# Sums on every partition by one product with ones, and a power of all elements on POOL, in two norms of a hybrid layer

## The chip, the cores and the metric

The kernel runs on one core of a Trainium2 chip. A time is the device time of one execution in microseconds (us); the number quoted for a kernel is the median of its runs. One further execution of the kernel was recorded by the hardware profiler, and every row below is from that one. The engines go by the names of the profile: PE is the matrix engine (PEld its weight load), DVE the vector engine, ACT the scalar engine, POOL the GpSimd engine, SP the engine that issues the weight DMAs.

## The reference, cut to what matters

One step of a layer with two mixers and an MLP, on 16 meta, 256 prompt and 64 sample tokens, D_MODEL = 2048. Two norms are touched by the change:

```python
def _rmsnorm(x, w):
    xf = x.astype(jnp.float32)
    xf = xf * lax.rsqrt(jnp.mean(xf * xf, axis=-1, keepdims=True) + EPS)
    return (xf * w.astype(jnp.float32)).astype(x.dtype)

# in _layer: the gated norm of the SSD mixer, one mean for each token and each of 4 groups of 512
ya = ya.reshape(b, l, SSD_D_INNER) * jax.nn.silu(z_a.astype(f32))
ya = _rmsnorm(ya.reshape(b, l, SSD_GROUPS, -1), ssd_norm_w.reshape(SSD_GROUPS, -1)).reshape(b, l, SSD_D_INNER)
...
# the norm ahead of the MLP, one mean for each token over 2048
hid = jnp.square(jax.nn.relu(_rmsnorm(h, norm_mlp_w) @ w_up))
h = h + hid @ w_down
```

## The kernel before, in words

Activations lie with channels on the 128 partitions and tokens along the free dimension. The weights, most of the 340.57 MB that the kernel reads, stream through once, in chunks of 512 rows by 256 columns. For each chunk `wsplit` (L201) makes two rounded halves: ACT copies the chunk to `hi`, DVE subtracts to get `lo`. `block` (L213) then runs 24 products on PE for the chunk (8 tiles, three products each: hi by x-high, hi by x-low, lo by x-high). `raw`, `hi` and `lo` have three buffers each, so the halves of a chunk can be made once the chunk three places earlier is used up, and two chunks lie ready ahead of PE at the most. Results go to `pbig`, a PSUM pool of four banks; a block fills two of them.

PE's order is written out by hand (L73). `run` (L240) interleaves a main generator (projections: the weight stream) with a side generator (scans and norms): what the side yields is the stretch of main work, in us, that PE does before it goes on with the side. The other engines' order is fixed when the kernel is built: a list planner takes, of the instructions that are ready by its own prices, the one that is earliest in the program. On the chip each engine runs its queue strictly in that order.

**The group norm.** `scan_ssd` (L608) runs for four groups, each beside the projections of the next. It goes through three chunks of tokens (64, 128 and 128 output tokens, c = 0, 1, 2). For a chunk it makes decay factors `em` (DVE, ACT, then POOL multiplies by `cb`), the state update (`xw` and `xwr` on DVE, `ph` on PE) and the output `yz` (`pyd` on PE). Then come squares (`sq`), which POOL adds up to one [128, tokens] tile, a yield, and `rstd_bcast` (L594). There PE sums over the partitions with a product by one column of ones, so that the tokens come to lie on the partitions and the sum is one column; DVE scales it; POOL raises this one column to -0.5 (L600); DVE multiplies the identity by it (L602, `dg`). A second yield follows, and PE spreads the diagonal over all partitions by a product with ones (`prb`). DVE then scales the four tiles of `yz` from PSUM (L67), ACT and DVE write `yh` and `yl`, the operands of the output projection. The yields place the next chunk's products (`pcb`, `pxt`, `ph`, `pyd`) at fixed distances behind.

**The MLP norm.** `mlp_rstd` (L1094) runs beside `mlp_first`, the first two blocks of the up projection, which fill all four `pbig` banks. It sums squares in `h2`, and does the same as above for three sets of 128 tokens: six PE passes, a power of a [128, 4] tile, three diagonals, six PE passes, and an ACT copy to `rbc` [128, 320]. `hidden` (L1132) then reads `pbig` and `rbc` on DVE (`hf`), and this is what frees a bank for the third block.

`conv` (L397), which runs for the projections of x, B, C, q, k and v, has short copies on POOL, products on DVE and copies on ACT.

Of the kernel before, what the change touches and what calls it, by code (L numbers as in the profile page):

```python
# [8 lines left out]
F32 = mybir.dt.float32  # L9
F32R = mybir.dt.float32r  # L10
AF = mybir.ActivationFunctionType
ALU = mybir.AluOpType
AX = mybir.AxisListType

P = 128
D = 2048
# [6 lines left out]
NO = NPR + NSA  # L23
DFF = 4 * D
EPS = 1e-6
# [17 lines left out]
def tile_hybrid_step(ctx: ExitStack, tc: tile.TileContext, i: dict, o: dict):  # L43
# [10 lines left out]
    def scr(name):  # L54
        return pss.tile([P, 512], F32, tag="sc", name=name)

    def mm(out, lhsT, rhs, start=True, stop=True, **kw):
        nc.tensor.matmul(out, lhsT=lhsT, rhs=rhs, start=start, stop=stop, **kw)  # L58

    def act(out, in_, func=AF.Copy, **kw):  # L60
        nc.scalar.activation(out=out, in_=in_, func=func, **kw)  # L61

    def tt(eng, out, a, b, op):
        eng.tensor_tensor(out=out, in0=a, in1=b, op=op)  # L64
# [4 lines left out]
    V, G = nc.vector, nc.gpsimd  # L69
    MUL, ADD, SUB = ALU.mult, ALU.add, ALU.subtract  # L70
# [5 lines left out]
    ident = const.tile([P, P], F32, name="ident")  # L76
    make_identity(nc, ident)
    ones = const.tile([P, P], F32, name="ones")
# [3 lines left out]
    nhalf_pow = const.tile([P, 4], F32, name="nhalf_pow")  # L82
    G.memset(nhalf_pow, -0.5)

    def transp(out, in_):
        n = in_.shape[0]
        nc.tensor.transpose(out, in_, ident[:n, :n])
# [418 lines left out]
    for n in range(2):  # L506
        w, wr = wt[:, n * 8:(n + 1) * 8, :], wpool.tile([P, 8, P], F32R, tag="hi", name="wtr", bufs=3)
# [83 lines left out]
    def new_y():  # L591
        return (cpool.tile([P, 4, NO], F32R, tag="yh", name="yh"), cpool.tile([P, 4, NO], F32R, tag="yl", name="yl"))

    def rstd_bcast(pool, ssum, n, width, wait):  # L594

        pc = scr("prs")
        mm(pc[:n, 256:257], ssum[:, :n], ones[:, 0:1])
        r = pool.tile([P, 1], F32, tag="r1", name="r1", bufs=2)
        V.tensor_scalar(out=r[:n], in0=pc[:n, 256:257], scalar1=1.0 / width, scalar2=EPS, op0=MUL, op1=ADD)
        tt(G, r[:n], r[:n], nhalf_pow[:n, 0:1], ALU.pow)  # L600
        dg = pool.tile([P, P], F32, tag="dg", name="dg", bufs=2)
        V.tensor_scalar(out=dg[:n, :n], in0=ident[:n, :n], scalar1=r[:n, 0:1], scalar2=None, op0=MUL)  # L602
        yield wait
        pr = scr("prb")
        mm(pr[:, :n], ones[:n, :], dg[:n, :n])
        return pr[:, :n]

    def scan_ssd(g, sg, x4, bc, z4):  # L608
        gh = slice(g * 8, (g + 1) * 8)
# [15 lines left out]
        ps = scr("psi")  # L625
# [8 lines left out]
        for c in range(3):  # L634
            lo, n, l0, nl, o0 = CH_LO[c], CH_N[c], L_LO[c], L_N[c], O_LO[c]
# [3 lines left out]
            ps = scr("pcb")  # L639
# [6 lines left out]
            pcb, ps = ps, scr("pxt")  # L646
# [39 lines left out]
            if c:  # L686
                po = scr("pyo")
                pov = po.rearrange("p (t l) -> p t l", l=nl)
                for t in range(4):
                    w = slice(t * P, (t + 1) * P)  # L690
# [17 lines left out]
                tt(V, yz[:, :, :nl], yz[:, :, :nl], pd, ADD)  # L708

            tt(G, yz[:, :, :nl], yz[:, :, :nl], z4[:, :, o0:o0 + nl], MUL)  # L710
            nx = max(nl, 96)
            sq = sg.tile([P, 4, P], F32, tag="sq", name="sq", bufs=1)
            if nl < nx:
                G.memset(sq[:, 0, nl:nx], 0.0)
            act(sq[:, :, :nl], yz[:, :, :nl], AF.Square)
            tt(G, sq[:, 0:2, :nl], sq[:, 0:2, :nl], sq[:, 2:4, :nl], ADD)
            tt(G, sq[:, 0, :nl], sq[:, 0, :nl], sq[:, 1, :nl], ADD)
            yield (5.4, 7.6, 7.0)[c]
            rb = yield from rstd_bcast(sg, sq[:, 0, :], nx, 512, (3.2, 5.2, 3.6)[c])
            rb = rb[:, :nl]  # L720
            yh, yl = ys[g] = ys.get(g) or new_y()
            for t in range(4):
                stt(yz[:, t, :nl], yz[:, t, :nl], par[:, SN + g * 4 + t:SN + g * 4 + t + 1], rb, MUL, MUL)
            act(yh[:, :, o0:o0 + nl], yz[:, :, :nl])
            tt(V, yl[:, :, o0:o0 + nl], yz[:, :, :nl], yh[:, :, o0:o0 + nl].bitcast(F32), SUB)
            if c == 2:
                for h, dst in zip(new, (o["ssd_p"], o["ssd_s"])):
                    ps = scr("pso")
                    for t in range(4):
                        transp(ps[:, t * P:(t + 1) * P], h[:, t * P:(t + 1) * P])  # L730
                    st = sg.tile([P, 4, P], F32, tag="sio", name="sio", bufs=2)
                    act(st, ps)
                    nc.sync.dma_start(dst[0, 0, gh].rearrange("(t h) p n -> (h p) t n", h=2), st)
                    yield 1.0
# [322 lines left out]
    with ExitStack() as sctx:  # L1057
        sg = sctx.enter_context(tc.tile_pool(name="sg", bufs=1))
        run(kept(proj_ssd(1), tiles), scan_ssd(0, sg, *tiles[0]))
        run(chain(out_a(0), kept(proj_ssd(2), tiles)), scan_ssd(1, sg, *tiles[1]))  # L1060
        run(chain(out_a(1), kept(proj_ssd(3), tiles)), scan_ssd(2, sg, *tiles[2]))
        run(chain(out_a(2), kept(proj_gdn(0), tiles)), scan_ssd(3, sg, *tiles[3]))
    with ExitStack() as sctx:
        sg = sctx.enter_context(tc.tile_pool(name="sgg", bufs=1))
# [6 lines left out]
        h2 = const.tile([P, NO], F32, name="h2")  # L1071
# [19 lines left out]
    mp = ctx.enter_context(tc.tile_pool(name="mp", bufs=1))  # L1091
    rbc = mp.tile([P, NO], F32, name="rbc")

    def mlp_rstd():  # L1094

        toks = ((0, 0), (128, 0), (192, 64))
        yield 5.0
        for k in range(KD):
            q = h2 if k == 0 else mp.tile([P, NO], F32, tag="hf", name="q", bufs=3)
            act(q, acc[:, k, :], AF.Square)  # L1100
            if k:
                tt(V, h2, h2, q, ADD)
            yield 0.9
        pc = scr("prs")
        r = mp.tile([P, 4], F32, name="rm")
        G.memset(r, 1.0)
        for n, (t0, _) in enumerate(toks):
            mm(pc[:, n:n + 1], h2[:, t0:t0 + P], ones[:, 0:1])
        V.tensor_scalar(out=r[:, 0:3], in0=pc[:, 0:3], scalar1=1.0 / D, scalar2=EPS, op0=MUL, op1=ADD)
        tt(G, r, r, nhalf_pow, ALU.pow)  # L1110
        pr = scr("prb")
        yield 3.5
        for n, (t0, d) in enumerate(toks):
            dg = mp.tile([P, P], F32, tag="dg", name="dg", bufs=3)
            V.tensor_scalar(out=dg, in0=ident, scalar1=r[:, n:n + 1], scalar2=None, op0=MUL)
            mm(pr[:, t0 + d:t0 + P], ones, dg[:, d:])
        act(rbc, pr[:, :NO])

    def conv_states():
        for r in range(6):  # L1120
# [35 lines left out]
    toks = ((0, slice(0, P), 0), (P, slice(0, P), P), (192, slice(64, P), 256))  # L1156
# [32 lines left out]
    for q in range(NQ):  # L1189
        hid[q] = (mp.tile([P, 16, NO], F32R, tag="hh", name="hh"), mp.tile([P, 16, NO], F32R, tag="hl", name="hl"))  # L1190
        pts = []
        if q == 0:
            run(kept(mlp_first(), pts), mlp_rstd())
            pts = pts[0]
        for b in range(8):
            if b >= len(pts):
                run(kept(mlp_up(), pts), conv_states() if q == 0 and b == 4 else None)
            hidden(q, b, pts[b])
        if q == NQ - 1:
            final_tiles()  # L1200
        for b in range(8):
            last = q == NQ - 1 and b
            run(mlp_down(q, b), chain(final_cols(b - 1), *([final_sum()] if b == 7 else [])) if last else None)
    H = D // 2
    with tc.manual_schedule():
        for t in range(3):
            final_part(7, t)
            r, n = frs[:, t:t + 1], toks[t][1]
            stt(r[n], fss[n, t, 7:8], 1.0 / D, fsum[n, t:t + 1], MUL, ADD)
            tt(G, r[n], r[n], nhalf_pow[n, 0:1], ALU.pow)  # L1210
        for m in range(2):
            for t, (_, n, t0) in enumerate(toks):
                dst = o["y_prompt"][0, t0:t0 + P, :] if t < 2 else o["y_sample"][0]
                w, r = slice(m * H, (m + 1) * H), frs[n, t:t + 1]
# [36 lines left out]
```

## Time and profile before

| | |
|---|---|
| median of 3 runs | 2333.14 us (2331.46 to 2334.69) |
| the profiled execution | 2331.78 us |
| its span, from the first to the last instruction | 2330.1 us |
| PE busy | 2300.5 us (99%), granted clock 0.994 of full speed |
| DVE busy | 1360.9 us (58%) |
| ACT busy | 1064.6 us (46%) |
| POOL busy | 333.0 us (14%) |
| HBM read | 340.57 MB, 155 GB/s with the writes over the span |

How to read it: matmuls overlap in their pipeline, so a busy PE says that it was not waiting, not that it could not be faster. Busy shares are means over stages: in the SSD stage (120 to 525 us) DVE and POOL have far more to do than in the MLP (1410 us to the end). Idle time of an engine costs nothing unless PE waits for it. "[2.3 <-DVE c]" behind a row is the idle time ahead of it and what ended it.

### The profile page before, as it was taken

Reading aid. Unit: us, or ns where it says so; the run is one execution under the profiler, and the core shown is the slowest. Engines: PE = TensorE matmul, PEld = TensorE weight load, DVE = VectorE, ACT = ScalarE, POOL = GpSimd, SP = SyncE. Lnnn points to the kernel's source line nnn. Section 1 sums busy time; section 2 is a strip of 40 time slices with the busy share of each in tenths; the row PEclk is TensorE's granted clock in tenths of the full one; section 3 lists DMA queues with packets and bytes.
Section 4 is the critical chain, followed back from the end, with each engine's and each line's share of the span. In section 5 each row is a group of like instructions: output and inputs, shape, how many; then the busy total and the mean of one; then the engine's idle time right before and its main releaser. Section 6 shows DMA issues by size and latency. Waiting matters only on the chain.

```text
span 2330.1 us, 40632 instructions
## 1 busy us (share of the span) xinstructions
PE 2300.5 (99%) x16393; PEld 2278.1 (98%) x16393; DVE 1360.9 (58%) x2147; ACT 1064.6 (46%) x1830; POOL 333.0 (14%) x488
## 2 busy tenths in 40 slices
PE   7999999999999999999999999999999999999997
PEld 7999999999999999999999999999999999999997
DVE  6674858585865547658668467444444444444444
ACT  5655546455445545554554445433343244324433
POOL 3151505041211102212212110000000000000000
PEclk8999999999999999999999999999999999999999
DMA  7846555545575555555546644544554444445543
GB/s 194 225 121 188 143 159 150 159 135 173 156 200 170 148 164 139 154 150 144 156 148 165 170 142 145 154 149 151 148 154 149 150 148 151 154 146 153 168 141 117
DMA packets 411046, 362.87 MB, mean 156 GB/s; under 512 B 48329, under 2 KB 407834, under 8 KB 410394
## 3 DMA queue, kind: packets, MB, share of 16 engines
q1 hardware_dynamic: 410746, 360.15, 53.1%
q8 instruction: 128, 2.10, 0.4%
q14 instruction: 60, 0.49, 0.1%
q10 hardware_dynamic: 112, 0.13, 0.0%
HBM read 340.57 MB, written 19.66 MB: 155 GB/s over the span
## 4 chain that ended last, share of the span: by engine, by line
PE 91%; DVE 5%; DMA 2%; issue 1%; SPq 1%; ACT 0%; ACTq 0%; POOL 0%; DVEq 0%
PE pbig L58 84%; DVE lo L64 1%; PE po L58 1%; DMA em<-rowd 1%; DVE pr L64 1%; DVE ubt L858 1%; PE pS L58 0%; PE pw L58 0%; PE pyd L58 0%; DVE c L67 0%; PE pkk L58 0%; PE pqk L58 0%; PE ph L58 0%; DMA x<-in_x_sample_dram 0%; PE pyo L58 0%
## 5 line engine op out<-in xcount | busy, mean ns | idle before, releaser
L64 DVE TENSOR_TENSOR lo<-raw,hi 128x1024 fp32r<-128x1024 f32 x591 | 739.1, 1251 | 697.3 <-ACT hi L61 688.0
L61 ACT ACTIVATE hi<-raw 128x1024 fp32r<-128x1024 f32 x592 | 626.3, 1058 | 892.1 <-PE pbig L58 834.6
L58 PE MATMUL pbig<-uh,hi 128*128 128x320 f32 (+2 forms) x2176 | 688.9, 317 | 3.1 <-ACT uh L61 3.1
L58 PE MATMUL pbig<-ul,hi 128*128 128x320 f32 (+2 forms) x2176 | 681.9, 313 | 2.9 <-DVE ul L67 2.7
L58 PE MATMUL pbig<-uh,lo 128*128 128x320 f32 (+2 forms) x2176 | 680.8, 313 | 1.6 <-DVE lo L64 1.6
L58 PEld LDWEIGHTS pbig<-uh,hi 128*128 128x128 f32 x2176 | 410.9, 189 | 9.1 <-ACT uh L61 3.8
L58 PEld LDWEIGHTS pbig<-ul,hi 128*128 128x128 f32 x2176 | 410.8, 189 | 4.7 <-DVE ul L67 4.3
L58 PEld LDWEIGHTS pbig<-uh,lo 128*128 128x128 f32 x2176 | 411.0, 189 | 2.4 <-DVE lo L64 2.4
L58 PE MATMUL pbig<-hh,hi 128*128 128x320 f32 x1024 | 318.0, 311 | 0.0
L58 PE MATMUL pbig<-hnl,hi 128*128 128x320 f32 x1024 | 317.1, 310 | 0.0
L58 PE MATMUL pbig<-hl,hi 128*128 128x320 f32 x1024 | 316.3, 309 | 0.0
L58 PE MATMUL pbig<-hh,lo 128*128 128x320 f32 x1024 | 316.2, 309 | 0.0
L58 PE MATMUL pbig<-hnh,lo 128*128 128x320 f32 x1024 | 315.8, 308 | 0.0
L58 PE MATMUL pbig<-hnh,hi 128*128 128x320 f32 x1024 | 315.1, 308 | 0.0
L58 PEld LDWEIGHTS pbig<-hnh,lo 128*128 128x128 f32 x1024 | 192.9, 188 | 0.0
L58 PEld LDWEIGHTS pbig<-hl,hi 128*128 128x128 f32 x1024 | 192.6, 188 | 0.0
L58 PEld LDWEIGHTS pbig<-hh,hi 128*128 128x128 f32 x1024 | 192.6, 188 | 0.0
L58 PEld LDWEIGHTS pbig<-hnh,hi 128*128 128x128 f32 x1024 | 192.4, 188 | 0.2
L58 PEld LDWEIGHTS pbig<-hh,lo 128*128 128x128 f32 x1024 | 192.5, 188 | 0.0
L58 PEld LDWEIGHTS pbig<-hnl,hi 128*128 128x128 f32 x1024 | 192.2, 188 | 0.0
L58 PE MATMUL pbig<-yh,hi 128*128 128x320 f32 x512 | 161.1, 315 | 0.0
L58 PE MATMUL pbig<-yh,lo 128*128 128x320 f32 x512 | 157.5, 308 | 0.0
(303 smaller groups left out, 2425.8 us busy)
## 6 DMA issues: line engine op xcount, KB each, us to landing
raw<-in_w_in_dram SPq DMA_DIRECT2D x256, 512.0 KB, 3.8
raw<-in_w_up_dram SPq DMA_DIRECT2D x128, 512.0 KB, 3.8
raw<-in_w_down_dram SPq DMA_DIRECT2D x128, 512.0 KB, 3.4
raw<-in_w_out_dram SPq DMA_DIRECT2D x64, 512.0 KB, 3.4
raw<-in_w_in_dram SPq DMA_DIRECT2D x32, 256.0 KB, 3.1
em<-rowd SPq DMA_DIRECT2D x8, 512.0 KB
u<-uD SPq DMA_DIRECT2D x4, 768.0 KB, 7.1
eab<-rowd SPq DMA_DIRECT2D x8, 336.0 KB, 6.9
```

The lines of the kernel that those rows point to most:

```text
L58: nc.tensor.matmul(out, lhsT=lhsT, rhs=rhs, start=start, stop=stop, **kw)
L61: nc.scalar.activation(out=out, in_=in_, func=func, **kw)
L64: eng.tensor_tensor(out=out, in0=a, in1=b, op=op)
L858: V.tensor_reduce(out=ubt[:NE, j0:, s], in_=v, axis=AX.X, op=ADD)
```

## The change

`rstd_bcast` becomes `rstd`. One product with the full 128 x 128 matrix of ones leaves the sum of each token on every partition at once, as a [128, tokens] tile in PSUM. DVE scales it and adds EPS into SBUF, and POOL raises all its elements to -0.5. The diagonal, the second product, the yield between them and the memset that padded 64 tokens to 96 are gone; DVE reads the factor from SBUF and not from PSUM. The second yield is kept, behind the writes of `yh` and `yl`. The MLP norm calls the same function for 320 tokens; its three sums, three diagonals, the yield of 3.5 and the ACT copy are gone.

```diff
-    def rstd_bcast(pool, ssum, n, width, wait):
-
-        pc = scr("prs")
-        mm(pc[:n, 256:257], ssum[:, :n], ones[:, 0:1])
-        r = pool.tile([P, 1], F32, tag="r1", name="r1", bufs=2)
-        V.tensor_scalar(out=r[:n], in0=pc[:n, 256:257], scalar1=1.0 / width, scalar2=EPS, op0=MUL, op1=ADD)
-        tt(G, r[:n], r[:n], nhalf_pow[:n, 0:1], ALU.pow)
-        dg = pool.tile([P, P], F32, tag="dg", name="dg", bufs=2)
-        V.tensor_scalar(out=dg[:n, :n], in0=ident[:n, :n], scalar1=r[:n, 0:1], scalar2=None, op0=MUL)
-        yield wait
-        pr = scr("prb")
-        mm(pr[:, :n], ones[:n, :], dg[:n, :n])
-        return pr[:, :n]
+    def rstd(out, sums, width):
+
+        w = sums.shape[1]
+        ps = scr("prb")
+        mm(ps[:, :w], ones, sums)
+        V.tensor_scalar(out=out, in0=ps[:, :w], scalar1=1.0 / width, scalar2=EPS, op0=MUL, op1=ADD)
+        tt(G, out, out, nhalf_pow[:, 0:1].to_broadcast([P, w]), ALU.pow)
...
             yield (5.4, 7.6, 7.0)[c]
-            rb = yield from rstd_bcast(sg, sq[:, 0, :], nx, 512, (3.2, 5.2, 3.6)[c])
-            rb = rb[:, :nl]
+            rb = sg.tile([P, P], F32, tag="dg", name="rb", bufs=2)[:, :nl]
+            rstd(rb, sq[:, 0, :nl], 512)
             yh, yl = ys[g] = ys.get(g) or new_y()
             for t in range(4):
                 stt(yz[:, t, :nl], yz[:, t, :nl], par[:, SN + g * 4 + t:SN + g * 4 + t + 1], rb, MUL, MUL)
             act(yh[:, :, o0:o0 + nl], yz[:, :, :nl])
             tt(V, yl[:, :, o0:o0 + nl], yz[:, :, :nl], yh[:, :, o0:o0 + nl].bitcast(F32), SUB)
+            yield (3.2, 5.2, 3.6)[c]
...
-        pc = scr("prs")
-        r = mp.tile([P, 4], F32, name="rm")
-        G.memset(r, 1.0)
-        for n, (t0, _) in enumerate(toks):
-            mm(pc[:, n:n + 1], h2[:, t0:t0 + P], ones[:, 0:1])
-        V.tensor_scalar(out=r[:, 0:3], in0=pc[:, 0:3], scalar1=1.0 / D, scalar2=EPS, op0=MUL, op1=ADD)
-        tt(G, r, r, nhalf_pow, ALU.pow)
-        pr = scr("prb")
-        yield 3.5
-        for n, (t0, d) in enumerate(toks):
-            dg = mp.tile([P, P], F32, tag="dg", name="dg", bufs=3)
-            V.tensor_scalar(out=dg, in0=ident, scalar1=r[:, n:n + 1], scalar2=None, op0=MUL)
-            mm(pr[:, t0 + d:t0 + P], ones, dg[:, d:])
-        act(rbc, pr[:, :NO])
+        rstd(rbc, h2, D)
```

## Rows read from the trace of the kernel before

**Rows 1.** The page: busy share of PE, and the chain by engine.
```profile
PE 2300.5 (99%) x16393; PEld 2278.1 (98%) x16393; DVE 1360.9 (58%) x2147; ACT 1064.6 (46%) x1830; POOL 333.0 (14%) x488
...
PE 91%; DVE 5%; DMA 2%; issue 1%; SPq 1%; ACT 0%; ACTq 0%; POOL 0%; DVEq 0%
```

**Rows 2.** POOL's groups by form: count | busy us, mean ns | idle before, releaser.
```profile
L64 POOL TENSOR_TENSOR sq<-sq 128x128 f32<-128x128 f32 x12 | 6.0, 499 | 2.4 <-ACT sq L61 2.1
...
L64 POOL TENSOR_TENSOR r<-r,nhalf_pow 128x1 f32<-128x1 f32 x8 | 4.4, 551 | 10.6 <-DVE r L599 10.4
...
L64 POOL TENSOR_TENSOR rm<-rm,nhalf_pow 128x4 f32<-128x4 f32 x1 | 1.0, 1014 | 20.4 <-DVE rm L1109 20.4
```

**Rows 3.** DVE's waits: waiter, releaser, us in total, times, longest.
```profile
DVE lo L64 <- ACT hi L61: 688.0, 424, 8.1
...
DVE on L64 <- POOL so L64: 10.2, 9, 1.2
...
DVE dg L602 <- POOL r L64: 5.6, 9, 0.7
```

**Rows 4.** Timeline of POOL, groups 0 and 1: start, us, instruction.
```profile
190.20 0.56 POOL L64 TENSOR_TENSOR r<-r,nhalf_pow 128x1 f32<-128x1 f32 x1 [0.38 <-DVE r L599]
...
235.53 0.55 POOL L64 TENSOR_TENSOR r<-r,nhalf_pow 96x1 f32<-96x1 f32 x1 [4.65 <-DVE r L599]
...
259.44 0.55 POOL L64 TENSOR_TENSOR r<-r,nhalf_pow 128x1 f32<-128x1 f32 x1 [2.53 <-DVE r L599]
...
271.85 3.53 POOL L64 TENSOR_TENSOR em<-em,cb 128x512 f32<-128x512 f32 x2
...
290.17 0.55 POOL L64 TENSOR_TENSOR r<-r,nhalf_pow 128x1 f32<-128x1 f32 x1
```

**Rows 5.** Timeline of DVE, group 1, around the three norms.
```profile
237.47 1.23 DVE L64 TENSOR_TENSOR lo<-raw,hi 128x1024 fp32r<-128x1024 f32 x1 [1.09 <-ACT hi L61]
...
260.94 2.36 DVE L64 TENSOR_TENSOR lo<-raw,hi 128x1024 fp32r<-128x1024 f32 x2 [0.63 <-ACT hi L61]
...
266.88 1.11 DVE L67 SCALAR_TENSOR_TENSOR yz<-yz,par,prb 128x128 f32<-128x128 f32 x4
...
292.13 1.22 DVE L64 TENSOR_TENSOR lo<-raw,hi 128x1024 fp32r<-128x1024 f32 x1
```

**Rows 6.** Timeline of ACT, group 1: splits that begin where PE ends a chunk.
```profile
243.67 1.06 ACT L61 ACTIVATE hi<-raw 128x1024 fp32r<-128x1024 f32 x1 [2.74 <-PE pbig L58]
...
264.49 1.06 ACT L61 ACTIVATE hi<-raw 128x1024 fp32r<-128x1024 f32 x1 [0.48 <-PE pbig L58]
...
298.59 1.06 ACT L61 ACTIVATE hi<-raw 128x1024 fp32r<-128x1024 f32 x1 [0.37 <-ACT z L61]
```

**Rows 7.** Timeline of DVE at the MLP norm.
```profile
1431.84 0.16 DVE L1109 TENSOR_SCALAR rm<-prs 128x3 f32<-128x3 f32 x1 [2.42 <-PE prs L58]
...
1437.04 1.28 DVE L67 SCALAR_TENSOR_TENSOR hf<-pbig,rbc 128x320 f32<-128x320 f32 x3
```

**Rows 8.** Timeline of PE at the MLP norm: the sums.
```profile
1431.00 0.72 PE L58 MATMUL prs<-ones,h 128*128 128x1 f32 x6
```

**Rows 9.** Timeline of ACT in the MLP: the split at a chunk's end.
```profile
1442.49 1.06 ACT L61 ACTIVATE hi<-raw 128x1024 fp32r<-128x1024 f32 x1 [0.81 <-PE pbig L58]
```

**Rows 10.** The chain in order of time: its longest piece in the MLP.
```profile
1474.39 740.14 PE pbig L58 x5055
```

**Rows 11.** Windows at the start: PE, PEld, DVE, ACT, POOL busy, PEclk, DMA, GB/s.
```profile
40.00:44.00 4.00, 3.25 (x11) 2.71 (x11) 2.11 (x5) 2.11 (x5) 0.00 (x0) 0.50 1.13 214
44.00:48.00 4.00, 3.09 (x18) 2.91 (x17) 1.35 (x3) 1.55 (x4) 0.52 (x2) 0.84 1.09 274
```

**Rows 12.** Timeline of PE: a stall ahead of these windows, and two products of groups 0, 1.
```profile
37.10 0.42 PE L58 MATMUL pbig<-ul,hi 128*128 128x336 f32 x1 [2.07 <-DVE ul L67]
...
199.47 0.30 PE L58 MATMUL pbig<-yh,hi 128*128 128x320 f32 x1
...
278.90 1.04 PE L58 MATMUL pyd<-em,xt 128*64 128x128 f32 x16
```

More of the change, by code (lines that the diff above doesn't have):

```diff
@@ L710, in scan_ssd @@
             tt(G, yz[:, :, :nl], yz[:, :, :nl], z4[:, :, o0:o0 + nl], MUL)
-            nx = max(nl, 96)
             sq = sg.tile([P, 4, P], F32, tag="sq", name="sq", bufs=1)
-            if nl < nx:
-                G.memset(sq[:, 0, nl:nx], 0.0)
             act(sq[:, :, :nl], yz[:, :, :nl], AF.Square)
@@ L1094, in mlp_rstd @@
     def mlp_rstd():
-        toks = ((0, 0), (128, 0), (192, 64))
         yield 5.0
```

## The prediction

> **What bounds the kernel now.** I read the page's busy shares and chain first. PE is busy for 99% of the span and is 91% of the chain that ended last [rows 1]: the kernel runs as fast as PE gets its operands, and whatever makes PE wait is paid in full. PE is fed by DVE and ACT, which split each weight chunk shortly before it is used. In the table of waits, DVE sits idle for 688 us ahead of `lo`, and all of that ends with ACT's `hi` [rows 3], which itself starts when PE frees a buffer. So the splitters are ahead, but only by the two chunks that three buffers allow. That is the cover that any new wait on DVE has, and the reader is to keep it in mind: a few us, not tens.
>
> **POOL's power, the new cost.** Next I read POOL's groups by form. The power of one column takes 551 ns, that of four columns 1014 ns, both on 128 partitions [rows 2]. The difference is 463 ns for three columns: 154 ns a column, and 397 ns that don't depend on the width. The add of 128 columns on the same engine takes 499 ns, at most 3.9 ns a column, so it is the power itself that is slow. The change raises 64, 128, 128 columns in each of four groups, and 320 once. No row shows a power wider than 4 columns, so both ends are kept: along the line of the two rows 64 columns take 10.3 us, 128 take 20.1 us and 320 take 49.8 us; at the price of the add they take 0.5 us or less, and 1.25 us for 320. I take the line, since its rows are of this very operation, and since work that has to be repeated for each column is what a steady 154 ns looks like.
>
> The Trainium skill speaks against this: GPSIMD Engine Reference, section "Elementwise — side-by-side cycle accounting", puts a two-input elementwise operation at about 2.6 cycles an element at 1.2 GHz, whatever it computes. By that, as an estimate, the powers would take about 0.3 us for 128 columns and 0.7 us for 320, and the sum would end as in the last rival below. The trace agrees for the add (499 ns) and not for the power (551 to 1014 ns for three columns more); the measurement decides.
>
> **Who waits for it.** The four scalings of `yz` on DVE read the result. What stands between them and the scaling of the sums in DVE's queue is set by the planner's price for a power. The waits show that this price is low: of the results that DVE waits for from POOL, the powers are the ones. `on` waits 10.2 us in 9 of 12 cases, 1.1 us each, and `dg` 5.6 us in 9 of 12 [rows 3], each about the whole of the power ahead of it; the planner put nothing between. So I expect the scalings right behind, and DVE standing still for nearly all of the power. Behind them in DVE's queue are the next `lo` (PE waits for it), the products of `conv`, and the next chunk's `xw` and `xwr` (PE's `ph`). Behind the power on POOL are the next chunk's `em` by `cb` (PE's `pyd`) and the short copies of `conv`. ACT's `yh` waits too, with `hi` behind it.
>
> **The group norm, priced in group 1.** A chunk is due at PE when PE ends the one before it, and that instant is seen where ACT begins a later `hi`.
> - 64 columns: the power starts at 235.5 [rows 4] and ends at 245.8. With about 0.9 us for four scalings and 1.2 us for the next `lo`, which stood at 237.5 [rows 5], that `lo` is done at 248.0. Its chunk is due at 243.6 [rows 6]: 4.4 us late. `xwr` is delayed too and can add up to 3 us; I take 5.
> - 128 columns, second chunk: 259.4 plus 20.1 is 279.6 [rows 4]; with 1.1 us for the scalings and 1.2 for the `lo` that stood at 260.9 [rows 5] it is 281.9, against 264.5 [rows 6]: 17.4 us.
> - 128 columns, third chunk: 290.2 plus 20.1 plus 2.3 is 312.6, and the `lo` of 292.1 [rows 5] is due at 298.6 [rows 6]: 14.0 us.
>
> That is 36.4, rounded to 37 us a group for what else slips, and 148 us for four. At the low end (one `lo` slips in ahead of the scalings each time) every case gets some 4 us cheaper, 110 us in all; at the high end DVE's whole idle time arrives at PE, 50 us a group and 200 in all.
>
> **The MLP norm.** The sums are ready for DVE at 1431.8 [rows 7]. Scaling 320 columns takes about 0.5 us (a `hf` of that width takes 0.43), so the power runs from 1432.4 to 1482.2. The first `hf` frees a bank at 1482.8. PE can finish two blocks meanwhile and no more, because they hold all four banks. The third block begins one chunk before 1442.5 [rows 9]; a chunk is 24 products of 0.146 us (740.14 us for 5055) [rows 10], so 1439.0, and 0.7 us earlier without the passes dropped. The stall is 44.5 us. Before, `hf` came at 1437.0, just ahead of PE, so none of this was paid.
>
> **PE's work and its clock.** Six short passes take 0.72 us [rows 8], 0.12 each. Each chunk drops two of four passes, 24 in all, 2.9 us; the MLP norm drops about 0.7 us. DVE loses `dg`, ACT the copy of `rbc`; both lie beside PE and are worth nothing. Together -3.6 us.
>
> After a stall PE has run slower before. At the start the granted clock was 0.50 from 40 to 44 and 0.84 from 44 to 48 [rows 11], that is, at 1.2 GHz and not 2.4 for a while, behind a wait of 2.07 us that ended at 37.1 [rows 12]. 4 us at half speed lose 2.0 us and the next window 0.6: 2.6 us for each stall. With 13 stalls that is 34 us; at the least 0, if the products of a stall's ends keep it up.
>
> **The sum.** 148 + 44.5 + 34 - 3.6 is 223 us. On the profiled execution's own time, 2331.8, that gives 2555; the median of the runs shown lies 1.4 us above it, so 2556. Its own range is 2510 to 2605.
>
> **Rivals.**
> - *The planner prices the power near its length, or other work comes first, and DVE doesn't stand.* For it: DVE waits were 1 us in length, too short to show much. Against it: nothing was put into them. Then only POOL is blocked. `em` by `cb`, 3.53 us [rows 4], starts at 279.6 and ends at 283.1, and `pyd` wants it at 278.9 [rows 12]: 4.2 us, in four groups 17. In group 0 the output projection begins at 199.5 [rows 12], and the power from 190.2 [rows 4] ends at 210.3, with 2.4 us (an estimate) for scaling and conversion: 13.2 us. The later groups have a projection between. The MLP stall stays, and six stalls cost 15.6 us of clock: 17 + 13.2 + 44.5 + 15.6 - 3.6 is 87, so 2420 (2395 to 2450).
> - *The power gets cheaper with width*, say a third of the slope. 128 columns take 7.0 us, 320 take 16.9. Then the second chunk is late by 259.4 + 7.0 + 2.3 - 264.5 = 4.2 us and the third by 0.9, 20 us in four groups; the MLP stalls 11.6 us; five stalls cost 13 us of clock. In all 41 us: 2374 (2345 to 2400). For it: two rows are no proof of a line to 128. Against it: nothing in them bends.
> - *The power costs what the add costs* (the skill's rule). Every result is there in about a microsecond, inside the cover, and the passes dropped remain: -3.6 us, 2330, not slower. It decides from where the power of 128 columns stays under some 3 us, since the nearest due time leaves 264.5 - 259.4 less 2.3 us. Against it is the step from 551 to 1014 ns.
>
> **Chances.** 0.58 for the forecast, 0.20 for the blocked POOL alone, 0.14 for the cheaper width, 0.08 for the price of the add. A change under 0.2% (4.7 us) can't be told from none here. The last rival's gain of 0.15% lies within it, and I split it 0.03 faster, 0.05 same; all else is slower, 0.92. The range reaches from 2370, leaving out that rival and half of the cheaper width, to 2610.
>
> **What would show it.** The profile after should have POOL powers of about 10, 20 and 50 us, some 244 us more POOL busy time (4 times 50.5, plus 49.8, less the old 7.6); DVE's `yz` waiting for POOL about 8, 18, 18 us; PE waiting for `lo` in the SSD stage and for DVE's `hf` near 1440 for about 45 us; granted clock at 0.5 behind these stalls. Wrong would be: powers of a microsecond; powers as long as said with `lo` filling DVE's queue ahead of `yz`; or PE short of its banks at another place than the MLP.

## The result: 2576.8 us, 10.5% slower, as forecast

The kernel after takes 2576.79 us (median of 4 runs, 2574.14 to 2579.15) against 2333.39 us (4 runs, 2331.46 to 2334.69) of the kernel before in the same comparison: a ratio of 1.1047, 95% interval 1.1034 to 1.1061. The forecast was 2556 us with a range of 2370 to 2610. The profiled execution of the kernel after took 2575.72 us, with a span of 2573.9 us and a mean granted clock of 0.952 (before: 2331.78, 2330.1, 0.994).

**The page.** Busy shares first, then the granted clock in 40 slices, then the chain that ended last, by engine; they answer to [rows 1].

```profile
PE 2326.4 (90%) x16359; PEld 2298.8 (89%) x16359; DVE 1363.0 (53%) x2132; ACT 1063.0 (41%) x1829; POOL 582.2 (23%) x483
...
PEclk9988888789889999999999999799999999999999
...
PE 80%; POOL 10%; DVE 5%; DMA 2%; issue 1%; ACT 1%; SPq 0%; ACTq 0%; DVEq 0%; POOLq 0%
```

PE fell from 99% to 90% of the span, and POOL, which had no share of the chain, now holds 10% of it. POOL is busy for 249 us more. PE is busy for 25.9 us more although it runs 34 matmuls fewer; the digits below 9 in the clock's row stand in the group-norm stage and at the MLP norm.

**POOL's groups by form**, which answer to [rows 2]: count | busy us, mean ns | idle before, releaser.

```profile
L64 POOL TENSOR_TENSOR rb<-rb,nhalf_pow 128x128 f32<-128x128 f32 x8 | 165.9, 20732 | 13.0 <-DVE rb L599 13.0
L64 POOL TENSOR_TENSOR rbc<-rbc,nhalf_pow 128x320 f32<-128x320 f32 x1 | 51.3, 51340 | 48.5 <-DVE rbc L599 48.5
L64 POOL TENSOR_TENSOR rb<-rb,nhalf_pow 128x64 f32<-128x64 f32 x4 | 42.4, 10595 | 15.6 <-DVE rb L599 15.6
```

From 64 to 128 columns the power grows by 158 ns a column, from 128 to 320 by 159. The two short rows had given 154; the line holds, up to eighty times the width it was read from.

**DVE's waits**, which answer to [rows 3]: waiter, releaser, us in total, times, longest.

```profile
DVE lo L64 <- ACT hi L61: 676.4, 421, 8.5
DVE yz L67 <- POOL rb L64: 204.1, 12, 20.9
...
DVE hf L67 <- POOL rbc L64: 51.5, 1, 51.5
```

All twelve group-norm powers and the MLP's one are waited for, nearly in full: 208.2 us of group-norm powers, 204.1 us of waiting. In eight of the twelve nothing stands in DVE's queue between the scaling of the sums and the scalings that read the result. In the other four it is a short piece of `c` or `em`, 0.5 to 0.65 us; in group 0's third chunk DVE also waits 2.9 us for a DMA of `em` there, inside the power.

**PE's waits**, the view that prices this. In the kernel after:

```profile
PE pbig L58 <- DVE lo L64: 111.2, 9, 17.0
PE pbig L58 <- DVE hf L67: 47.2, 1, 47.2
PE ph L58 <- ACT xwr L61: 40.3, 4, 10.7
...
PE pbig L58 <- ACT yh L61: 13.5, 1, 13.5
PE ph L58 <- DVE xwr L64: 4.8, 4, 2.8
```

In the kernel before, the same two kinds that occur there:

```profile
PE pbig L58 <- DVE lo L64: 1.6, 3, 0.7
...
PE ph L58 <- DVE xwr L64: 1.0, 2, 0.6
```

One operand is late for each power: four first chunks at `ph` (through ACT's and DVE's `xwr`), four second and three third chunks at `lo`, group 0's third chunk at `yh`, where the output projection begins, and the MLP at `hf`. That is 13 stalls and some 214 us of new waiting; the experiment e3 shows that 4.8 us of it, at `ph`, come without a power too.

**One stall followed through: the first chunk of group 1.** POOL, then DVE, then PE, from their timelines: start, us, instruction, idle before it and what ended it.

```profile
285.10 10.53 POOL L64 TENSOR_TENSOR rb<-rb,nhalf_pow 128x64 f32<-128x64 f32 x1 [4.49 <-DVE rb L599]
```

```profile
284.80 0.22 DVE L599 TENSOR_SCALAR rb<-prb 128x64 f32<-128x64 f32 x1
295.67 0.87 DVE L67 SCALAR_TENSOR_TENSOR yz<-yz,par,rb 128x64 f32<-128x64 f32 x4 [10.64 <-POOL rb L64]
...
301.16 1.91 DVE L64 TENSOR_TENSOR lo<-raw,hi 128x1024 fp32r<-128x1024 f32 x1
303.00 1.74 DVE L64 TENSOR_TENSOR xwr<-xw,xwr 128x512 fp32r<-128x512 f32 x1
```

```profile
301.16 0.80 PE L58 MATMUL ph<-xwr,bt 128*128 128x512 f32 x1 [9.35 <-ACT xwr L61]
304.80 1.22 PE L58 MATMUL ph<-xwr,bt 128*128 128x512 f32 x2 [2.84 <-DVE xwr L64]
```

DVE scales the sums at 284.80 and does nothing for 10.64 us. It then has the scalings, two `lo`, the products of `xw`, and `xwr` to do in its queue's order, and PE wants `xwr` first. Nearly the whole of DVE's idle time arrives at PE, as 9.35 us at the first product. The 2.84 us at the second have another cause: the `lo` of 301.16 stands ahead of DVE's `xwr`, and e3, which has no power, waits 2.92 us at this place. The windows of PE around it (length, busy time and matmuls, granted clock, DMA share, GB/s):

```profile
290.00:295.00 5.00, 1.81 (x12) 1.00 0.00 0
295.00:300.00 5.00, 0.00 (x0) 0.64 0.00 0
300.00:305.00 5.00, 1.00 (x2) 0.50 0.46 118
305.00:310.00 5.00, 5.00 (x17) 0.50 0.26 92
```

While PE stands, the granted clock falls to 0.50, 1.2 GHz, and PE's first 6 us of work behind the stall run at that level: 3.0 us lost.

**The second chunk of group 1**, DVE and then PE:

```profile
323.68 0.29 DVE L599 TENSOR_SCALAR rb<-prb 128x128 f32<-128x128 f32 x1 [0.61 <-PE prb L58]
344.81 0.35 DVE L67 SCALAR_TENSOR_TENSOR yz<-yz,par,rb 128x128 f32<-128x128 f32 x1 [20.84 <-POOL rb L64]
345.08 1.22 DVE L64 TENSOR_TENSOR lo<-raw,hi 128x1024 fp32r<-128x1024 f32 x1
```

```profile
346.35 0.65 PE L58 MATMUL pbig<-uh,lo 128*128 128x336 f32 x1 [16.84 <-DVE lo L64]
```

Here PE still had split weights ahead, so 4 of DVE's 20.84 us were covered.

**The MLP norm**, DVE, POOL and PE, and two windows behind it; they answer to [rows 7] to [rows 9]:

```profile
1627.68 0.48 DVE L599 TENSOR_SCALAR rbc<-prb 128x320 f32<-128x320 f32 x1
1679.71 0.89 DVE L67 SCALAR_TENSOR_TENSOR hf<-pbig,rbc 128x320 f32<-128x320 f32 x2 [51.54 <-POOL rbc L64]
```

```profile
1628.34 51.34 POOL L64 TENSOR_TENSOR rbc<-rbc,nhalf_pow 128x320 f32<-128x320 f32 x1 [48.49 <-DVE rbc L599]
```

```profile
1680.35 0.61 PE L58 MATMUL pbig<-hnh,hi 128*128 128x320 f32 x1 [47.21 <-DVE hf L67]
```

```profile
1680.00:1684.00 4.00, 3.65 (x14) 0.50 0.00 0
1684.00:1688.00 4.00, 4.00 (x24) 0.80 0.66 189
```

PE goes on for 4.8 us of the power (1628.34 to 1633.14), until its four banks are full, and stands for the rest. Behind it, 3.65 us at 0.50 lose 1.8 and 4 us at 0.80 lose 0.8: 2.6 us.

### The profile page after: what moved, and what is told of

It is laid out like the page before. It is cut to its first block, busy times and chain, and to the rows that moved or that the text cites. A ratio compares the mean times of both kernels' runs of the same rounds, so it can differ in the third digit from the quotient of the medians.

```text
span 2573.9 us, 40546 instructions
## 1 busy us (share of the span) xinstructions
PE 2326.4 (90%) x16359; PEld 2298.8 (89%) x16359; DVE 1363.0 (53%) x2132; ACT 1063.0 (41%) x1829; POOL 582.2 (23%) x483
## 4 chain that ended last, share of the span: by engine, by line
PE 80%; POOL 10%; DVE 5%; DMA 2%; issue 1%; ACT 1%; SPq 0%; ACTq 0%; DVEq 0%; POOLq 0%
PE pbig L58 74%; POOL rb L64 8%; POOL rbc L64 2%; DVE lo L64 2%; DMA em<-rowd 1%; PE po L58 1%; DVE c L67 1%; PE ph L58 0%; PE pS L58 0%; PE pw L58 0%; DVE em L658 0%; PE pkk L58 0%; PE pqk L58 0%; DVE ul L67 0%; PE pyd L58 0%
## 5 line engine op out<-in xcount | busy, mean ns | idle before, releaser
L58 PE MATMUL pbig<-uh,lo 128*128 128x320 f32 (+2 forms) x2176 | 688.7, 316 | 111.2 <-DVE lo L64 111.2
L58 PEld LDWEIGHTS pbig<-uh,lo 128*128 128x128 f32 x2176 | 417.1, 192 | 113.8 <-DVE lo L64 113.8
L58 PEld LDWEIGHTS pbig<-uh,hi 128*128 128x128 f32 x2176 | 417.1, 192 | 9.7 <-ACT uh L61 4.4
L58 PEld LDWEIGHTS pbig<-ul,hi 128*128 128x128 f32 x2176 | 416.9, 192 | 6.4 <-DVE ul L67 5.8
L58 PE MATMUL pbig<-hnh,hi 128*128 128x320 f32 x1024 | 316.6, 309 | 47.2 <-DVE hf L67 47.2
L64 POOL TENSOR_TENSOR rb<-rb,nhalf_pow 128x128 f32<-128x128 f32 (+1 forms) x12 | 208.2, 17353 | 28.6 <-DVE rb L599 28.6
```

## The experiments

My theory: POOL's power grows with its columns, DVE's queue stands for it because the scalings are right behind, and PE pays for what exceeds its cover, with some 2.6 us of clock for each stall. The main rivals: POOL alone blocked, which would cost the same whether or not DVE waits; and that the sums by PE or the changed queues are to blame, not the power.

**e1_mlp_only: only the MLP norm changed.** The kernel before with the new function used in the MLP alone.

```
-        pc = scr("prs")
...
-        act(rbc, pr[:, :NO])
+        rstd(rbc, h2, D)
```

> The kernel before with the new function in the MLP norm alone; the group norm stays as before. Theory 1 (DVE's queue stands behind the power, PE runs out of banks or halves, and runs at half clock for a while after it): 2333.4 us plus a stall of 47 us before the third block, plus 2.6 us of clock, less 0.7 us of passes: 2382 us (2376 to 2388). Theory 2 (POOL is occupied, and its own later work comes late): POOL has no other work in the MLP, so within 5 us of before, 2333.

Measured 2381.23 us against 2332.05, 1.0210 (1.0194 to 1.0226): 49.2 us, of which PE waits 47.2 for `hf`, once. That is within what I expected, so the mechanism and the size of this part are shown.

**e2_group_only: only the group norm changed.**

```
-        rstd(rbc, h2, D)
+        pc = scr("prs")
...
+        act(rbc, pr[:, :NO])
```

> The kernel after with the old function in the MLP norm. If the parts add up, this is the changed kernel's 2576.8 us less the 49 us of the MLP part: 2528 us (2520 to 2536). If the parts share a cost (a clock that stays low, a backlog carried from one to the other), the sum of the two gains over before differs from 243 us by more than 10 us.

Measured 2526.42 us, 1.0833 (1.0819 to 1.0848): 194.4 us. With e1's 49.2 it makes 243.6, and the whole change costs 243.4: the two halves add up.

**e3_mult_for_power: all as after, but POOL multiplies where it raised.** It leaves the norms' values out: the scale of the sums is a constant.

```
-        V.tensor_scalar(out=out, in0=ps[:, :w], scalar1=1.0 / width, scalar2=EPS, op0=MUL, op1=ADD)
-        tt(G, out, out, nhalf_pow[:, 0:1].to_broadcast([P, w]), ALU.pow)
+        V.tensor_scalar(out=out, in0=ps[:, :w], scalar1=1e-30, scalar2=1e-3, op0=MUL, op1=ADD)
+        tt(G, out, out, nhalf_pow[:, 0:1].to_broadcast([P, w]), MUL)
```

> The kernel after with a multiplication on POOL in place of the power, at the same place, shape and operands; the norms' values are not computed (the scale of the sums is a constant). Theories 1 and 2 both put the whole loss on the length of the power: 2333.4 less 3.6 us for the dropped passes, 2330 us (2325 to 2334). Rival 3 (the rest of the change costs: the wide product with ones, the DVE scaling out of PSUM, the factor read from SBUF, the moved yield): over 2340 us.

Measured 2333.44 us (11 runs), 1.0006 (0.9997 to 1.0014): no difference that can be measured, and at the upper end of what I expected. POOL's groups, and PE's line of the page:

```profile
L64 POOL TENSOR_TENSOR rb<-rb,nhalf_pow 128x128 f32<-128x128 f32 x8 | 3.2, 400 | 14.5 <-DVE rb L599 14.5
```

```profile
PE 2292.8 (98%) x16359; PEld 2270.8 (97%) x16359; DVE 1362.3 (58%) x2132; ACT 1063.9 (46%) x1829; POOL 325.2 (14%) x483
```

Same tile, same operands, same engine: 400 ns for a product, 20732 for a power. The whole loss is the power's length; the rest of the change comes out level, neither dearer nor cheaper. PE is busy for 7.7 us less than before, but 4.0 of these lie in the first 60 us, ahead of any norm, where the two executions ran at different granted clocks (0.83 before, 0.89 here). From 60 us on PE is busy for 2249.7 us against 2253.3: 3.6 less, just what the dropped passes were priced at. Against that it waits for `xwr` at `ph` 5.8 us in five places, where it waited 1.0 before, and the span is 0.9 us longer. Half of these 5.8 us are one place in group 1, where DVE's queue has another order. First the kernel before, then e3:

```profile
241.31 1.18 DVE L64 TENSOR_TENSOR xwr<-xw,xwr 128x512 fp32r<-128x512 f32 x1
242.41 2.31 DVE L64 TENSOR_TENSOR lo<-raw,hi 128x1024 fp32r<-128x1024 f32 x1
```

```profile
242.10 1.93 DVE L64 TENSOR_TENSOR lo<-raw,hi 128x1024 fp32r<-128x1024 f32 x1
243.96 1.75 DVE L64 TENSOR_TENSOR xwr<-xw,xwr 128x512 fp32r<-128x512 f32 x1
```

The planner, which fixes DVE's order when a kernel is built, has put a `lo` ahead of `xwr` here.

**e4_power_unread: the power is taken, but nobody reads it.** The scalings read DVE's tile, so DVE never waits for POOL's result. The norms leave the power out, and the scale of the sums is a constant, as in e3.

```
-        V.tensor_scalar(out=out, in0=ps[:, :w], scalar1=1.0 / width, scalar2=EPS, op0=MUL, op1=ADD)
-        tt(G, out, out, nhalf_pow[:, 0:1].to_broadcast([P, w]), ALU.pow)
+        V.tensor_scalar(out=out, in0=ps[:, :w], scalar1=1e-30, scalar2=1e-3, op0=MUL, op1=ADD)
+        tt(G, unread, out, nhalf_pow[:, 0:1].to_broadcast([P, w]), ALU.pow)
```

> The kernel after, where the scalings read DVE's result directly and POOL raises the same elements into a tile that nothing reads; the norms leave the power out. POOL is as busy as in the changed kernel, DVE waits for none of it. Theory 1: only the next chunk's em by cb is late, 4.2 us in the third chunk of four groups, with some clock: 2333.4 + 17 + 10 - 3.6 = 2357 us (2330 to 2375). Theory 2: most of the loss of the group norm stays, over 2480 us.

Measured 2373.14 us, 1.0174 (1.0160 to 1.0188): 41 us, where the whole change costs 243. PE's waits:

```profile
PE pyd L58 <- POOL em L64: 23.2, 13, 4.9
PE pbig L58 <- DVE lo L64: 6.9, 3, 5.6
```

POOL as a blocked engine is real: a power from 270.87 to 291.60 holds the next chunk's `em` until 292.18, and `pyd` waits. But it is a sixth of the loss; the rest, some 200 us, needs the read of the result by DVE. The time lay 16 us above the middle value expected: `pyd` waits in 13 places, 23.2 us, not in the four groups' one each, 17 us, that I had priced; one `lo` is 5.6 us late; and PE is busy for 17.7 us more than in e3 from 60 us on, where I had put 10 for the clock.

**e5_act_sqrt: ACT takes the root, DVE the reciprocal.** POOL is out of the norm.

```
-        V.tensor_scalar(out=out, in0=ps[:, :w], scalar1=1.0 / width, scalar2=EPS, op0=MUL, op1=ADD)
-        tt(G, out, out, nhalf_pow[:, 0:1].to_broadcast([P, w]), ALU.pow)
+        act(out, ps[:, :w], AF.Sqrt, scale=1.0 / width, bias=eps)
+        V.reciprocal(out, out)
```

> The kernel after with the root on ACT (square root straight out of PSUM, scale and EPS in the same instruction) and a reciprocal on DVE, in place of DVE's scaling and POOL's power; the result is the same. Theories 1 and 2: nothing long is left between the sums and the scalings, so like the kernel with a multiplication for the power, 2333 us (2330 to 2337); ACT's table loads, 1.28 us each in the trace of before, lie inside its idle time. Rival 3 (wide elements are dear on any engine, or table loads delay hi): over 2345 us.

A miss: 2345.12 us, 1.0057 (1.0044 to 1.0069), 8 us above the end of what I expected and just on the price of rival 3, which this run alone does not exclude (e8 does). ACT's group of table loads, and PE's waits:

```profile
L61 ACT ACT_TABLE_LOAD x65 | 83.4, 1283 | 7.1 <-DMA em<-rowd 4.4 <-PE pbig L58 0.8 <-PEq L1220 0.8
```

```profile
PE ph L58 <- DVE xwr L64: 8.2, 6, 3.0
...
PE ph L58 <- ACT xwr L61: 4.1, 3, 1.5
```

There are 16 table loads more than the 49 of before, 1.28 us each, and DVE's reciprocal of 128 columns takes 949 ns. `ph` waits 12.3 us in nine places against 5.8 in five of e3, and from 60 us on PE is busy 8.3 us longer than in e3 at the same matmuls (2258.0 against 2249.7); in the stretch from 60 to 540 us the granted clock is 0.98 against 1.00.

**e6_scalings_later: as after, but a chunk's scalings come one chunk later.** They are emitted ahead of the next chunk's sums, behind the latest `lo` (the last chunk's 16.5 us later). The power and the result stay.

```
+            scale_held()
             rb = sg.tile([P, P], F32, tag="dg", name="rb", bufs=2)[:, :nl]
             rstd(rb, sq[:, 0, :nl], 512)
...
-            for t in range(4):
-                stt(yz[:, t, :nl], yz[:, t, :nl], par[:, SN + g * 4 + t:SN + g * 4 + t + 1], rb, MUL, MUL)
...
+            held.append((yz, rb, nl, o0))
...
+        yield 16.5
+        scale_held()
```

> The kernel after, where the scalings of a chunk are emitted ahead of the next chunk's sums (for the last chunk 16.5 us of main work later) and tied behind the latest lo in DVE's queue; the power, its width and the result stay. Theory 1 (what costs is the place of the scalings in DVE's queue): the group norm costs what the unread power cost, 41 us, plus 13.5 us in group 0, whose output projection waits for yh, and the MLP's 49 us stay: 2332 + 41 + 13.5 + 49 = 2436 us (2415 to 2455). Theory 2 (POOL's length itself): over 2540 us.

Measured 2436.40 us, 1.0448 (1.0432 to 1.0464): 140 us of the change's 243 are back, with every power as long as it was. PE's waits:

```profile
PE pbig L58 <- DVE hf L67: 47.2, 1, 47.2
PE pyd L58 <- POOL em L64: 23.8, 5, 6.4
PE pbig L58 <- ACT yh L61: 17.2, 3, 15.0
```

The waits for `lo` (1.4 us, as in e3) and `xwr` are gone; what is left is the MLP, the blocked `em`, and `yh` of the output projection. So 140 of the 194 us that the group norm costs were DVE standing in order behind the power.

**e7_32_columns: POOL raises only the first 32 columns.** The other columns keep a constant scale, and the norms' values are left out.

```
-        V.tensor_scalar(out=out, in0=ps[:, :w], scalar1=1.0 / width, scalar2=EPS, op0=MUL, op1=ADD)
+        V.tensor_scalar(out=out, in0=ps[:, :w], scalar1=1e-30, scalar2=1.0, op0=MUL, op1=ADD)
-        tt(G, out, out, nhalf_pow[:, 0:1].to_broadcast([P, w]), ALU.pow)
+        tt(G, out[:, :32], out[:, :32], nhalf_pow[:, 0:1].to_broadcast([P, 32]), ALU.pow)
```

> The kernel after, where POOL raises only the first 32 columns in each norm (the others are left as DVE's scaling made them, and that scale is a constant): 397 + 32 x 158 ns = 5.5 us a power. Theory 1 with a cover that differs by place (none for the first chunk, whose ph waited 10.3 us for a power of 10.6; 3.7 us for the second, whose lo waited 17.0 of 20.7; over 6 for the third; 4.1 in the MLP): 4 x 5.2 + 4 x 1.8 + 1.4 us and four stalls of 2.6 us of clock on 2333 us: 2373 us (2355 to 2385). Rival (every us of power costs a us, without cover): 2333 + 13 x 5.5 = 2405 us.

Measured 2383.00 us, 1.0217 (1.0203 to 1.0231), inside what I expected and 10 us above its middle. The power's row of its tile (min, median, max ns) and PE's waits:

```profile
L64 POOL TENSOR_TENSOR rb<-rb,nhalf_pow x12: 5426/5427/5692, 137.4 to 568.2; 128x32 f32<-128x32 f32 x12
```

```profile
PE ph L58 <- ACT xwr L61: 21.6, 5, 5.7
PE pbig L58 <- DVE lo L64: 10.1, 11, 1.7
PE ph L58 <- DVE xwr L64: 8.1, 7, 2.8
```

At 5.4 us `lo` hardly waits any more: its cover holds for nearly this long. `ph` has none: its four first chunks still wait about 5 us each for ACT's `xwr` (4.6 to 5.7), the length of the power. The clock took more than I had priced: from 60 us on PE is busy for 16.4 us more than in e3, against four stalls of 2.6.

**e8_act_sqrt_later: e5 with the scalings of the first two chunks moved as in e6.** It joins what e5 and e6 pointed to and leaves nothing out.

```
+        act(out, ps[:, :w], AF.Sqrt, scale=1.0 / width, bias=eps)
+        V.reciprocal(out, out)
...
+            held.append((yz, rb, nl, o0))
+            if c == 2:
+                scale_held()
```

> The kernel with the root on ACT and a reciprocal on DVE, and the scalings of the first two chunks behind the next chunk's products (the last chunk's stay in place); the result is the same. In e5 PE waited 12.3 us for xwr at ph, 1.0 in the kernel before, and PE was busy 10 us longer than with the multiplication, at a lower clock. Theory 1 (DVE's and ACT's work between the sums and xwr is paid at ph, and the clock falls with each such wait): both go, 2345 - 11 - 10 = 2324 us, at the most 2330, and with the dropped passes a little faster than before (2332). Rival (the table loads on ACT delay hi, or the reciprocals make DVE late for lo): 2340 to 2350 us, and PE's waits end with lo or hi.

Measured 2329.72 us (11 runs, 2328.26 to 2331.13) against 2331.68 (21 runs): 0.9992 (0.9983 to 1.0000). Its last 2 us are at the edge of what can be measured, so I call it as fast as before. That is the slow end of what I expected (2324, at the most 2330). Against e5 it is 15.4 us faster with the same table loads and reciprocals. PE's waits for `xwr`:

```profile
PE ph L58 <- DVE xwr L64: 1.4, 2, 1.2
PE ph L58 <- ACT xwr L61: 0.8, 1, 0.8
```

So e5 did not lose by ACT's added 22 us (busy 1064.6 before, 1086.7 in e5, 1086.6 in e8), but by the place of the scalings, right behind a result that takes a table load (1.28), a root (0.37) and a reciprocal (0.95), 2.6 us, and by the order of DVE's queue that comes with that place. This excludes rival 3 of e5.

**e9_mult_later: e3 with the scalings moved as in e8.** As in e3, the norms' values are left out.

```
-        tt(G, out, out, nhalf_pow[:, 0:1].to_broadcast([P, w]), ALU.pow)
+        tt(G, out, out, nhalf_pow[:, 0:1].to_broadcast([P, w]), MUL)
...
+            held.append((yz, rb, nl, o0))
```

> The kernel with a multiplication in place of the power (the norms' values are not computed), with the scalings of the first two chunks behind the next chunk's products. The multiplication alone gave 2333.4 us, no gain for the 3.6 us of passes dropped, with 5.5 us of waits for xwr at ph. Theory 1 (these waits took the gain): 2329 us (2326 to 2331). Rival (the passes dropped were not worth anything, they lay under something else): 2332 to 2335 us with the waits gone.

Measured 2332.64 us (11 runs), 1.0002 (0.9993 to 1.0011): the time of e3, and that of the rival, but not with the waits gone as the rival had it. `ph` still waits 5.1 us in three places, groups 1 to 3, so these waits are not due to the scalings' place. In all three DVE has a second `lo`, of 1.9 us, between `xw` and `xwr`, as e3 has in group 1. The dropped passes are worth about what I priced (from 60 us on, PE is busy for 2251.0 us here and 2253.3 before), and the waits at `ph` take it back. In e8 DVE makes `xwr` in these groups ahead of the second `lo`, `ph` waits 2.2 us in all, PE is busy for 2250.5 us, and the span is 1.5 us shorter than before. Why the planner orders one kernel this way and another that way, no run shows.

## Why the prediction was right, term by term

| term of the sum | predicted us | measured us | from |
|---|---|---|---|
| group norm, first chunk (4) | 20 | 39.3 | waits for `xwr` at `ph`, less 5.8 of e3 |
| second and third chunk (4 each) | 126 | 123.1 | waits for `lo` and `yh`, less 1.6 of before |
| rounding up to 37 a group | 2 | | |
| MLP | 44.5 | 47.2 | wait for `hf` |
| clock | 34 | 32.0 | PE busy from 60 us on, after less e3 |
| dropped passes | -3.6 | -3.6 | PE busy from 60 us on, e3 less before |
| waits at `ph` without a power | 0 | 4.8 | e3 less before |
| the first 60 us and other waits | 0 | 1.0 | what is left of the span |
| sum | 223 | 243.8 | the spans |

PE's busy time is taken from 60 us on because the first 60 us, ahead of every norm, differ from trace to trace (47.1 us of it before, 43.1 in e3, 44.6 after).

- **Bound and cover.** Right: PE's waits, the lost clock and the dropped passes add up to the span's growth but for 1.0 us. "The two chunks that three buffers allow" held for `lo` (16.8 us of wait for 20.8 of DVE's). It did not hold for `xwr`.
- **The power.** Right. Taken 10.3, 20.1 and 49.8 us, measured 10.6, 20.7 and 51.3. The other end of the bounds, the price of the add, is excluded by these lengths, and e3's 400 ns for a product of the same shape shows that the operation is dear and not the shape. By the Trainium skill (GPSIMD Engine Reference, "Elementwise — side-by-side cycle accounting") about 2.6 cycles an element at 1.2 GHz would make an estimate of 0.3 us for 128 columns. The trace agrees roughly for the product (0.40) and not at all for the power (20.7). The section takes its figure from an add and calls it a floor for two inputs; it names no power, and "whatever it computes" was my reading of it.
- **Who waits.** Right, and tighter than said: no `lo` slips in, so `yz` waits 10.6, 20.8 and 20.3 us in group 1's three chunks, where I had written 8, 18 and 18. e6 shows that the queue's order is the cause; e4 shows that POOL's own delay is a sixth.
- **First chunk: the term that was mis-sized.** I priced 4.4 us at `lo` and "up to 3 us" for `xwr`, 5 in all. PE waited at `ph` instead: 39.3 us in four groups more than in e3, where I had 20. The products of `xw` and `xwr` are made after the scalings and used at once; there is no buffer ahead of `ph`. e7 shows it apart: at 5.4 us `lo` waits 1.7 at most, `ph` 5.7. With the 4.8 us at `ph` that come without a power, it is more than the whole 21 us between 223 and 243.8; the other terms miss by little and nearly cancel.
- **Second and third chunks.** Priced 17.4 and 14.0 in every group. PE waited 17.0, 16.8, 16.8 and 13.3 us in the second chunks, 15.6, 15.6 and 14.7 in three third ones, and 13.5 for `yh` in group 0's third, a place that I had named only in a rival. So the seconds came out shorter than priced and the thirds longer; that their sum is so near is in part luck.
- **MLP.** Priced 44.5, measured 47.2: 1.5 us from the power's length, 1.1 from the time in which PE still fills its banks (4.8 us and not 5.9).
- **Clock.** Priced 13 stalls of 2.6 us. From 60 us on PE's busy time is 32.0 us above that of e3 at the same matmuls, 2.5 a stall; the mean granted clock is 0.952 against 0.995. The price was read off two windows at the start, behind a wait of 2.07 us and with a second wait, of 0.76 us, inside them. That stalls of 9 to 47 us cost the same had no row behind it, so the nearness is in part luck.
- **Dropped passes.** Right in PE's busy time, 3.6 us. They are not seen in the time of e3 or e9, because the waits at `ph` that DVE's new order brings cost about as much. It decides no sign.
- **The low end.** Twelve cases cheaper by 4 us each take 48 from 148 and leave 100, not the 110 that the prediction has. Nothing hangs on it.
- **The rivals.** The price of the add falls by POOL's rows. POOL blocked alone falls by e4 and e6. The cheaper width falls by the line, and its price was too low besides: I gave 41 us for powers of 7.0 us on 128 columns, and e7 costs 51 at 5.4, for it too left `ph` uncovered.

## What to carry to other kernels

Two short rows of the same operation at different sizes give its slope, and that is worth more than any row of another operation on the engine: here a product and a power of one shape differ fiftyfold. A result that is read in order costs the reader's queue, so ask of each operand behind it how far ahead it is made; a buffer of two chunks covers microseconds, and an operand made and used in the same step covers nothing. Give each stall of the bounding engine the clock that it loses besides (2.5 us here), and where an operation can't be made shorter, move its reader behind other work: that alone gave back 140 of 243 us.

## What the runs showed of the hardware

The power on POOL stays on one line from 1 to 320 columns: 0.55, 1.01, 5.43, 10.60, 20.73 and 51.34 us for 1, 4, 32, 64, 128 and 320, about 158 ns a column. The root on ACT and the reciprocal on DVE (0.95 us for 128 columns, 2.15 for 320) are much the cheaper pair, although the thirteen roots among other functions brought 16 more table loads of 1.28 us. And short waits cost clock too: with none longer than 3.0 us at `ph`, e5 has PE busy 8.3 us longer than e3 from 60 us on at the same matmuls, with a granted clock of 0.98 against 1.00 between 60 and 540 us.
